# The low parts of projection weights in a split-precision block kernel: an accumulating DMA in place of a VectorE subtraction

## The chip, the cores and the metric

The kernel runs on one core of a Trainium2 chip. The metric is the device time of one execution in microseconds (us); lower is better. The kernel before takes 1429.39 us, the median of 3 runs (1428.5 to 1431.72).

## What is computed

One layer of a diffusion backbone on 1024 latent tokens and 256 context tokens with 1024 channels, all in float32: a modulated norm, one wide input projection `w_in`, a recurrent branch (8 heads) and a Fourier branch, a gated merge, an output projection, and a squared-ReLU MLP. Cut to what matters here:

```python
h_lat = modulate(rms_norm(x, g_mix), sh1, sc1)
ux_l, uy_l, uf_l, ug_l = split_in_cols(h_lat @ w_in)     # 1024 x (1024 | 1024 | 512 | 2048)
xc = depthwise_conv(ux, conv_w, conv_b)                  # per head of 128 channels:
h_l = bidir_rglru(xc_ctx, xc_lat, w_a, b_a, w_x, b_x, lam)   # gates from w_a, w_x, two scans
y_a = (h_l * gelu(uy)) @ w_lru_out
y_b = fourier_mix(uf) @ w_f_out
merged = sigmoid(ug)[:, :1024] * y_a + sigmoid(ug)[:, 1024:] * y_b
x = x + gt1 * (merged @ w_out)
x = x + gt2 * sq_relu_mlp(modulate(rms_norm(x, g_mlp), sh2, sc2), w1, w2)
```

## The kernel before

**Split operands.** The matmuls run on a rounded form of float32 (F32R). To keep the accuracy, each operand is split in two: a high part, which is the operand rounded by a ScalarE copy, and a low part, operand minus high part, by VectorE (`split`, lines 97-98). A product is then three matmul passes into one PSUM bank: weight high by input high, weight high by input low, and, last, weight low by input high (`passes`, line 151). So of each weight, the high part is wanted first and the low part after two passes.

**The stream of weights.** All 60 projection weights up to the merge come through one object, `weights` of class `Stream` (lines 107-137), in the order of the list at lines 139-149:

- four columns `WIN_UF` (the Fourier branch, "the Fourier weights"), seven gates `WIN_GA`, the first convolution weight `win[0]`, and the last `WIN_GA`;
- for each head: `wg` (the head's gate weights, 128 x 512), the convolution weight `win` of the **next** head, `WIN_UY` (the gelu branch), `wf` (Fourier output, 128 x 640), and `WIN_GB`;
- eight columns of `wlo`, the recurrent output projection.

Apart from `wg` and `wf` each is 128 x 1024, 512 KB. `ahead` keeps up to four raw weights loaded (SyncE's DMA queue, line 126, tiles `wr`) and up to three split (tiles `wh` and `wl`, rings of three buffers each); `take` hands out the next and calls `ahead` first. The `wr` ring of four buffers is shared with the gemv of the modulation vectors (`Gemvs.steps`, lines 269-280), which loads rows of `w_mod` there in the heads and multiplies them with VectorE (line 277 the first of a group, line 279 the others). So a weight's load may wait for a gemv step to free its buffer.

**What sets the order.** From line 395 to 443, the start-up, PE, VectorE and ScalarE run in the order in which the code stands (`tc.manual_schedule`): inputs are normalised, transposed and modulated (lines 381-393 hold the helpers), `weights.ahead` at lines 407, 408 and 413 splits the first three Fourier weights, and `uf_mm` (line 420) multiplies each input tile by these three, into the three PSUM buffers named `mm`. Those three buffers are all there are: the fourth Fourier weight is multiplied after it, by `mm_lat` (line 324), once `fourier_in` (line 471, ScalarE) has evacuated the first. Behind the start-up a scheduler sets the order of each engine when the program is built; `take` gives the loads and splits a priority 600 instructions ahead (`PRIO`). Each engine then runs its queue strictly in order, and waits where an operand or buffer is not ready.

**A head.** `gates` (line 613) multiplies the head's convolved input by four gate weights, and ScalarE evacuates each by a tanh (line 626 the latent part, 627 the context part; the context bank `smp` has two buffers, so PE waits at line 622 for 627 two gates before). `conv` of the next head (line 590) runs next on PE, by `lat_mm` (line 321), then `gelu_out` (658), gemv steps, and `fourier_out` (670), whose evacuation by VectorE stands at lines 702 and 703. Scans and gates' products (lines 640-656) are VectorE's.

Of the kernel before, what the change touches and what calls it, by code (L numbers as in the profile page):

```python
# [18 lines left out]
F32R = mybir.dt.float32r  # L19
BF16 = mybir.dt.bfloat16  # L20
I32 = mybir.dt.int32
AF = mybir.ActivationFunctionType
ALU = mybir.AluOpType
# [22 lines left out]
def f32(ap):  # L46
    return ap.bitcast(F32)
# [3 lines left out]
def block_kernel(es: ExitStack, tc: tile.TileContext, a, out):  # L51
    nc = tc.nc
    V, S, PE, G = nc.vector, nc.scalar, nc.tensor, nc.gpsimd
# [21 lines left out]
    def nm(s):  # L75
        uid[0] += 1
        return f"{s}_{uid[0]}"
# [13 lines left out]
    def wr_tile():  # L91
        return wp.tile([P, 1024], F32, tag="wr", name=nm("wr"))
# [4 lines left out]
    def split(src, hi, lo):  # L97
        return S.activation(hi, src, AF.Copy), V.tensor_tensor(lo, src, f32(hi), ALU.subtract)  # L98
# [8 lines left out]
    class Stream:  # L107
# [14 lines left out]
        def ahead(self, split_to=None, load_to=None):  # L122
            while len(self.raw) < min(self.i + 4 if load_to is None else load_to, len(self.items)):
                src, shape = self.items[len(self.raw)]
                r = wr_tile()[:, 0:shape[1] * shape[2]]
                dma(r, src)
                self.raw.append(r)
            while len(self.done) < min(self.i + 3 if split_to is None else split_to, len(self.items)):
                j = len(self.done)
                r, shape = self.raw[j], self.items[j][1]  # L130
                h, l = (wp.tile([P, 1024], F32R, tag=t, name=nm(t), bufs=n)[:, 0:shape[1] * shape[2]]
                        for t, n in (("wh", 3), ("wl", 3)))
                if shape[1] == 5:
                    V.tensor_tensor(r[:, 256:512], r[:, 0:256], r[:, 256:512], ALU.add)
                    V.scalar_tensor_tensor(r[:, 0:256], r[:, 0:256], 2.0, r[:, 256:512], ALU.mult, ALU.subtract)
                split(r, h, l)
                self.done.append([t.rearrange("p (a b) -> p a b", b=shape[2]) for t in (h, l)])

    W8 = (P, KT, P)
# [1251 lines left out]
```

## Time and profile before

| | |
|---|---|
| median of 3 runs | 1429.39 us (1428.5 to 1431.72) |
| profiled execution, its own time | 1429.25 us |
| its span on the core | 1427.4 us |
| mean granted clock of TensorE | 0.993 |
| PE busy (matmul) | 97% |
| VectorE (DVE) busy | 73% |
| ScalarE (ACT) busy | 42% |
| GpSimd (POOL) busy | 1% |
| DMA: by SyncE's queue | 191.53 MB, 38.3% of 16 engines' span |

The profile is of one execution, which took 1429.25 us; the span of its instructions, 1427.4 us, is what timelines and windows cover, counted from the span's start. Busy shares are averages over the whole span, so a place must be read from its own stretch. PEld is the loading of weights into the array beside the matmuls. An idle time is put down to the releaser that came last.

### The profile page before, as it was taken

To read this page: it belongs to the slowest core of one execution; us is meant where nothing else is said; L and a number is where in the kernel's file an instruction comes from. 1 tells how busy PE (TensorE), PEld (TensorE's weight loads), DVE (VectorE), ACT (ScalarE), POOL (GpSimd) and SP (SyncE) were. 2 spreads that over 40 slices of the span, in tenths; PEclk is the share of its full clock that TensorE was granted. 3 is DMA by queue.
4 is the path that set the end of the run, shared out by engine and by line. 5 is a ranking of instruction groups with operands and counts; after the bars stand their busy time and mean duration, and the time that the engine had idled before them with its cause. 6 is when DMAs were issued, how large, how long until landed. Compare 5 with 4: busy or idle time off the path is not lost.

```text
span 1427.4 us, 16255 instructions
## 1 busy us (share of the span) xinstructions
PE 1384.8 (97%) x6352; PEld 1129.5 (79%) x6352; DVE 1046.7 (73%) x1262; ACT 605.3 (42%) x755; POOL 13.8 (1%) x14
## 2 busy tenths in 40 slices
PE   4999999999999999999999899999999999999997
PEld 3888888888888887788877687888887888888885
DVE  7664557898779888854747877666665977969968
ACT  7452337755764666522125612222222544333512
POOL 0000000000000000000000200000000000000000
PEclk9999999999999999999999899999999999999999
DMA  8532711441344135454923233223326561340332
GB/s 336 194 118 67 255 60 60 135 140 66 109 135 134 46 120 171 161 168 164 333 89 133 74 134 132 95 98 118 118 91 238 187 226 63 124 149 1 101 150 104
DMA packets 64556, 192.57 MB, mean 135 GB/s; under 512 B 7203, under 2 KB 7611, under 8 KB 64479
## 3 DMA queue, kind: packets, MB, share of 16 engines
q1 hardware_dynamic: 64479, 191.53, 38.3%
q8 instruction: 50, 0.82, 0.2%
q14 instruction: 27, 0.22, 0.0%
HBM read 154.27 MB, written 37.23 MB: 134 GB/s over the span
## 4 chain that ended last, share of the span: by engine, by line
PE 85%; DVE 7%; ACT 3%; DMA 2%; issue 2%; SPq 0%; DVEq 0%; ACTq 0%
PE mm L321 25%; PE bk L922 19%; PE mm L1141 19%; PE mm L776 6%; PE mm L863 5%; PE mm L1218 3%; PE mm L621 2%; PE smp L596 2%; DVE pg L98 1%; DMA wr<-in_win 1%; ACT jk L217 1%; PE mm L686 1%; PE mm L497 1%; PE smp L622 1%; DVE l L653 1%
## 5 line engine op out<-in xcount | busy, mean ns | idle before, releaser
L321 PE MATMUL mm<-pg,wh 128*128 128x512 f32 x1120 | 309.4, 397 | 0.5 <-DVE pg L98 0.5
L321 PEld LDWEIGHTS mm<-pg,wh 128*128 128x128 f32 x1120 | 205.1, 189 | 43.9 <-DVE pg L98 1.0
L922 PE MATMUL bk<-pg,wh 128*128 128x512 f32 x720 | 228.7, 398 | 4.6 <-DVE pg L98 4.5
L321 PE MATMUL mm<-pg,wl 128*128 128x512 f32 x560 | 175.6, 395 | 0.0
L922 PEld LDWEIGHTS bk<-pg,wh 128*128 128x128 f32 x720 | 136.6, 190 | 38.7 <-DVE pg L98 5.7
L922 PE MATMUL bk<-pg,wl 128*128 128x512 f32 x360 | 143.7, 399 | 0.4 <-DVE wl L98 0.4
L98 DVE TENSOR_TENSOR wl<-wr,wh 128x1024 fp32r<-128x1024 f32 (+2 forms) x73 | 81.6, 1120 | 75.3 <-ACT wh L98 75.1
L98 ACT ACTIVATE wh<-wr 128x1024 fp32r<-128x1024 f32 (+2 forms) x73 | 71.0, 975 | 145.3 <-PE mm L321 67.0
L321 PEld LDWEIGHTS mm<-pg,wl 128*128 128x128 f32 x560 | 105.7, 189 | 24.4
L98 ACT ACTIVATE wh<-pg 128x1024 fp32r<-128x1024 f32 (+1 forms) x52 | 52.7, 1028 | 142.4 <-PE bk L922 52.7
L98 ACT ACTIVATE pg<-pg 128x1024 fp32r<-128x1024 f32 (+4 forms) x93 | 79.4, 884 | 45.8 <-DVE pg L1155 13.2
L98 DVE TENSOR_TENSOR pg<-pg,pg 128x1024 fp32r<-128x1024 f32 (+4 forms) x82 | 77.7, 980 | 24.1 <-ACT pg L98 23.9
L863 PE MATMUL mm<-pg,pg 128*128 128x512 f32 x384 | 92.3, 397 | 0.8 <-DVE g L1016 0.8
L863 PEld LDWEIGHTS mm<-pg,pg 128*128 128x128 f32 x384 | 71.1, 188 | 19.4 <-DVE g L1016 2.8
L922 PEld LDWEIGHTS bk<-pg,wl 128*128 128x128 f32 x360 | 68.5, 190 | 16.9 <-DVE wl L98 0.9
L98 DVE TENSOR_TENSOR wl<-pg,wh 128x1024 fp32r<-128x1024 f32 (+1 forms) x52 | 60.3, 1179 | 21.2 <-ACT wh L98 21.2
L1141 PE MATMUL mm<-pg,pg 128*128 128x512 f32 x240 | 74.1, 390 | 0.0
L776 PE MATMUL mm<-pg,wh 128*128 128x512 f32 x256 | 70.0, 394 | 1.7 <-ACT pg L98 1.7
L1155 DVE TENSOR_TENSOR pg<-pg,mm 128x1024 f32<-128x1024 f32 x34 | 41.0, 1220 | 39.0 <-PE mm L1141 37.8
L922 PE MATMUL bk<-pg,pg 128*128 128x512 f32 x264 | 64.8, 395 | 0.3 <-ACT pg L931 0.3
L1141 PE MATMUL mm<-pg 128*128 128x512 f32 x164 | 64.1, 391 | 0.0
L922 PEld LDWEIGHTS bk<-pg,pg 128*128 128x128 f32 x264 | 49.3, 188 | 12.1 <-ACT pg L931 0.5
(285 smaller groups left out, 2454.7 us busy)
## 6 DMA issues: line engine op xcount, KB each, us to landing
wr<-in_win SPq DMA_DIRECT2D x36, 512.0 KB, 4.5
pg<-act_d SPq DMA_DIRECT2D x70, 256.0 KB, 5.2
pg<-in_wm SPq DMA_DIRECT2D x32, 512.0 KB, 8.2
wr<-in_wm SPq DMA_DIRECT2D x32, 512.0 KB, 3.6
wr<-in_w SPq DMA_DIRECT2D x32, 512.0 KB, 3.5
act_d<-pg SPq DMA_DIRECT2D x32, 512.0 KB, 3.0
pg<-in_w SPq DMA_DIRECT2D x56, 256.0 KB, 5.3
pg<-in_x SPq DMA_DIRECT2D x16, 512.0 KB, 7.9
```

The costliest lines, as they stand in the source:

```text
L98: return S.activation(hi, src, AF.Copy), V.tensor_tensor(lo, src, f32(hi), ALU.subtract)
L217: S.activation(j[:, 0:src.shape[1]], src, AF.Square, accum_out=dst)
L321: PE.matmul(ps[:, h * HB:(h + 1) * HB], l[:, k, :], r[:, h * HB:(h + 1) * HB], start=k == 0 and i == 0, stop=k == KT - 1 and i == 2)
L497: PE.matmul(ps[:, o0:o0 + n1 - n0], l[:, q * P:(q + 1) * P], r[:, n0:n1], start=i == 0, stop=i == 2)
L596: PE.matmul(pc[:, 0:TC], l[:, k, :], r[:, k % 4, :], start=k == 0 and i == 0, stop=k == KT - 1 and i == 2)
L621: PE.matmul(ps[:, h * HB:(h + 1) * HB], l, r[:, h * HB:(h + 1) * HB], start=i == 0, stop=i == 2)
L776: PE.matmul(ps[:, h * HB:(h + 1) * HB], l[:, k, :], r[:, h * HB:(h + 1) * HB], start=k == 0 and i == 0, stop=k == KT - 1 and i == 2)
L863: PE.matmul(ps, l, r, start=k == 0 and j == 0, stop=k == KT - 1 and j == 2)
L922: PE.matmul(ps, l, r, start=first and k == 0 and i == 0, stop=k == 3 and i == 2, skip_group_check=not first)
L1141: PE.matmul(t[j], l, r, start=u not in self.ON and k == 0 and n == 0, stop=k == len(op) - 1 and n == 2, skip_group_check=u in self.ON)
L1155: V.tensor_tensor(t, t, ps, ALU.subtract if u in self.SUB else ALU.add)
L1218: PE.matmul(ps[h], l, r[:, h * HB:(h + 1) * HB], start=f == 0 and j == 0, stop=f == 2 * self.NPL - 1 and j == 2)
```

## The change

For the 52 weights that are not `wf`, the call of `split` is replaced. ScalarE makes the high part as before and then writes the negated weight, rounded the same way, into the low part's tile; a DMA on GpSimd's queue then adds the weight, read from DRAM a second time, onto that tile. The eight `wf`, which are combined by VectorE before they are split, stay as they are. Lines behind the change are five further down.

```diff
@@ Stream.ahead, -133,7 +133,12 @@
                 if shape[1] == 5:
                     V.tensor_tensor(r[:, 256:512], r[:, 0:256], r[:, 256:512], ALU.add)
                     V.scalar_tensor_tensor(r[:, 0:256], r[:, 0:256], 2.0, r[:, 256:512], ALU.mult, ALU.subtract)
-                split(r, h, l)
+                if shape[1] == 5:
+                    split(r, h, l)
+                else:
+                    S.activation(h, r, AF.Copy)
+                    S.activation(l, r, AF.Copy, scale=-1.0)
+                    G.dma_start(out=l, in_=self.items[j][0].rearrange("p a b -> p (a b)").bitcast(F32R), accum_op=ALU.add)
                 self.done.append([t.rearrange("p (a b) -> p a b", b=shape[2]) for t in (h, l)])
```

In the whole program VectorE loses 52 instructions (`TENSOR_TENSOR wl<-wr,wh`, 44 of 128x1024 and 8 of 128x512), ScalarE gains 52 of the same sizes, and POOL's queue gains 52 transfers of 512 KB (8 of them 256 KB).

ScalarE in the start-up, where the first three Fourier weights are split (`wr` raw weight, `wh` and `wl` its high and low part; `pg<-smp,mod` is the modulation of an input tile). Before:

```order
L98 ACTIVATE wh_292<-wr_171 128x1024
L98 ACTIVATE wh_296<-wr_173 128x1024
L388 ACTIVATE pg_310<-smp_282,mod 128x512
L98 ACTIVATE pg_95<-pg_310 128x512
L388 ACTIVATE pg_310<-smp_283,mod 128x512
L98 ACTIVATE pg_95<-pg_310 128x512
L98 ACTIVATE wh_328<-wr_175 128x1024
L388 ACTIVATE pg_335<-smp_318,mod 128x512
```

With the change, the same stretch:

```order
L139 ACTIVATE wh_292<-wr_171 128x1024
L140 ACTIVATE wl_293<-wr_171 128x1024
L139 ACTIVATE wh_297<-wr_173 128x1024
L140 ACTIVATE wl_298<-wr_173 128x1024
L393 ACTIVATE pg_312<-smp_282,mod 128x512
L98 ACTIVATE pg_95<-pg_312 128x512
L393 ACTIVATE pg_312<-smp_283,mod 128x512
L98 ACTIVATE pg_95<-pg_312 128x512
L139 ACTIVATE wh_330<-wr_175 128x1024
L140 ACTIVATE wl_331<-wr_175 128x1024
L393 ACTIVATE pg_338<-smp_320,mod 128x512
```

Each high part has its negation right behind it; two operations stand ahead of the first modulation, and three ahead of that of the second input tile.

ScalarE at the end of the start-up, where the fourth Fourier weight (`wr_599` before, `wr_602` now) is split and the three PSUM buffers `mm` are evacuated by `fourier_in` (line 471, now 476). Before:

```order
L98 ACTIVATE wh_603<-wr_599 128x1024
L471 ACTIVATE pg_662<-mm_342 128x1024
L98 ACTIVATE wh_609<-wr_601 128x1024
L98 ACTIVATE wh_670<-wr_607 128x1024
L471 ACTIVATE pg_664<-mm_343 128x1024
L471 ACTIVATE pg_666<-mm_344 128x1024
```

With the change:

```order
L139 ACTIVATE wh_606<-wr_602 128x1024
L140 ACTIVATE wl_607<-wr_602 128x1024
L139 ACTIVATE wh_613<-wr_604 128x1024
L139 ACTIVATE wh_675<-wr_611 128x1024
L140 ACTIVATE wl_614<-wr_604 128x1024
L140 ACTIVATE wl_676<-wr_611 128x1024
L476 ACTIVATE pg_667<-mm_345 128x1024
L476 ACTIVATE pg_669<-mm_346 128x1024
L476 ACTIVATE pg_671<-mm_347 128x1024
```

The first evacuation stood behind one split; it now stands behind the splits and negations of three weights.

VectorE in head 1, around the first gemv step of the head (`gacc<-wr,silu`, line 277, now 282), which frees a `wr` buffer (`l<-l,mm` at 128x255 to 257 is the evacuation of `fourier_out`, lines 702 and 703, now 707 and 708). Before:

```order
L662 SCALAR_TENSOR_TENSOR l_2022<-l_2022,mm_1973 128x1024
L656 TENSOR_TENSOR l_1849<-l_1849,l_1856 128x1024
L702 TENSOR_TENSOR l_2079<-l_2079,mm_2066 128x257
L703 TENSOR_TENSOR l_2079<-l_2079,mm_2066 128x255
L702 TENSOR_TENSOR l_2079<-l_2079,mm_2066 128x256
L703 TENSOR_TENSOR l_2079<-l_2079,mm_2066 128x256
L664 SCALAR_TENSOR_TENSOR l_2022<-l_2022,mm_1973 128x1024
L277 TENSOR_SCALAR gacc<-wr_2029,silu 128x1024
```

With the change:

```order
L661 TENSOR_TENSOR l_1865<-l_1865,l_1872 128x1024
L98 TENSOR_TENSOR l_1980<-l_1970,l_1979 128x1280
L667 SCALAR_TENSOR_TENSOR l_2039<-l_2039,mm_1990 128x1024
L282 TENSOR_SCALAR gacc<-wr_2046,silu 128x1024
L707 TENSOR_TENSOR l_2097<-l_2097,mm_2084 128x257
L708 TENSOR_TENSOR l_2097<-l_2097,mm_2084 128x255
L707 TENSOR_TENSOR l_2097<-l_2097,mm_2084 128x256
L708 TENSOR_TENSOR l_2097<-l_2097,mm_2084 128x256
L284 SCALAR_TENSOR_TENSOR gacc<-wr_2049,silu,gacc 128x1024
```

The first gemv step stood behind the four rows of the Fourier evacuation, and now stands ahead of them; the same in the other heads that have gemv steps.

## Rows read from the trace of the kernel before

**Rows 1.** Page, part 1: busy time, share of the span, instructions of each engine.

```profile
PE 1384.8 (97%) x6352; PEld 1129.5 (79%) x6352; DVE 1046.7 (73%) x1262; ACT 605.3 (42%) x755; POOL 13.8 (1%) x14
```

**Rows 2.** Windows: length, busy PE, PEld, DVE, ACT, POOL, then PEclk, DMA share, GB/s.

```profile
35.00:75.00 40.00, 39.48 (x206) 32.64 (x205) 25.86 (x42) 17.82 (x23) 0.00 (x0) 1.00 0.45 173
...
215.00:580.00 365.00, 361.11 (x1808) 301.61 (x1808) 305.33 (x294) 234.99 (x260) 0.00 (x0) 1.00 0.34 113
580.00:700.00 120.00, 118.29 (x510) 95.28 (x509) 71.55 (x78) 31.46 (x44) 0.00 (x0) 1.00 0.59 203
```

**Rows 3.** Waits of PE from 35 to 700 us: total, times, longest.

```profile
PE smp L622 <- ACT l L627: 2.6, 3, 1.5
PE mm L776 <- ACT pg L98: 1.7, 1, 1.7
PE smp L622 <- DVE wr L297: 1.3, 1, 1.3
```

**Rows 4.** Costs by line and form: count | busy, mean ns | idle before, releaser.

```profile
L98 DVE TENSOR_TENSOR wl<-wr,wh 128x1024 fp32r<-128x1024 f32 x57 | 69.5, 1222 | 67.2 <-ACT wh L98 67.0 <-DMA pg<-in_wm 0.2
L98 ACT ACTIVATE wh<-wr 128x1024 fp32r<-128x1024 f32 x57 | 60.1, 1057 | 120.1 <-DMA wr<-in_win 52.4 <-PE mm L321 41.8 <-issue 12.1
```

**Rows 5.** Page, part 6: DMA issues, KB each, median us to landing.

```profile
wr<-in_win SPq DMA_DIRECT2D x36, 512.0 KB, 4.5
...
pg<-in_wm SPq DMA_DIRECT2D x32, 512.0 KB, 8.2
wr<-in_wm SPq DMA_DIRECT2D x32, 512.0 KB, 3.6
```

**Rows 6.** Timeline of ACT, 24 to 50: start, us, instruction, [idle before].

```profile
26.35 1.99 ACT L98 ACTIVATE wh<-wr 128x1024 fp32r<-128x1024 f32 x2
30.22 0.78 ACT L388 ACTIVATE pg<-smp,mod 128x512 f32<-128x512 f32 x1 [1.87 <-DVE mod L261]
...
32.89 1.04 ACT L98 ACTIVATE wh<-wr 128x1024 fp32r<-128x1024 f32 x1
```

**Rows 7.** Timeline of PE, 24 to 50.

```profile
33.14 2.06 PE L321 MATMUL mm<-pg,wh 128*128 128x512 f32 x4
...
35.67 1.09 PE L321 MATMUL mm<-pg,wh 128*128 128x512 f32 x4
...
38.01 0.63 PE L321 MATMUL mm<-pg,wl 128*128 128x512 f32 x2
```

**Rows 8.** Timeline of ACT, 72 to 80.

```profile
73.67 1.06 ACT L98 ACTIVATE wh<-wr 128x1024 fp32r<-128x1024 f32 x1 [3.00 <-PE mm L321]
74.63 1.01 ACT L471 ACTIVATE pg<-mm 128x1024 f32<-128x1024 f32 x1
```

**Rows 9.** Timeline of PE, 73 to 79.

```profile
76.67 1.10 PE L321 MATMUL mm<-pg,wh 128*128 128x512 f32 x4
77.61 0.63 PE L321 MATMUL mm<-pg,wl 128*128 128x512 f32 x2
```

**Rows 10.** Timeline of ACT in head 1.

```profile
261.76 1.06 ACT L98 ACTIVATE wh<-wr 128x1024 fp32r<-128x1024 f32 x1 [6.95 <-DMA wr<-in_win]
```

**Rows 11.** Timeline of PE in head 1, the convolution's first low pass.

```profile
271.30 0.63 PE L321 MATMUL mm<-pg,wl 128*128 128x512 f32 x2
```

**Rows 12.** Timeline of DVE in head 1.

```profile
254.76 0.42 DVE L702 TENSOR_TENSOR l<-l,mm 128x257 f32<-128x257 f32 x1
...
257.21 0.75 DVE L277 TENSOR_SCALAR gacc<-wr,silu 128x1024 f32<-128x1024 f32 x1
```

**Rows 13.** Windows around a stop of PE behind the stretches above; columns of rows 2.

```profile
804.90:808.20 3.30, 0.00 (x0) 0.00 (x0) 3.30 (x4) 2.16 (x3) 1.65 (x1) 0.80 0.00 0
808.20:817.10 8.90, 7.66 (x17) 5.59 (x18) 7.23 (x10) 1.12 (x2) 0.00 (x0) 0.50 0.70 236
```

**Rows 14.** Timeline of PE, 591 to 598.

```profile
594.68 1.19 PE L776 MATMUL mm<-pg,wh 128*128 128x512 f32 x4 [1.71 <-ACT pg L98]
```

**Rows 15.** Timeline of DVE, 24 to 46.

```profile
38.48 1.53 DVE L249 SCALAR_TENSOR_TENSOR gacc<-pg,silu,gacc 128x512 f32<-128x512 f32 x2
```

## The prediction, made before the changed kernel had run

> **What bounds the kernel now.** I read the busy shares first, then the stretches in which the changed weights are used, then the costs of the operation removed, then the waits and timelines at the places where a low part is needed soonest. TensorE is busy for 97% of the span, VectorE for 73% and ScalarE for 42% [rows 1]. The stretches that use the 52 changed weights are fuller still: PE is busy for 39.48 of 40 us in the start-up, 361.11 of 365 in heads 1 to 6 and 118.29 of 120 with the last eight weights, while VectorE has 305 of 365 at most [rows 2]. So PE sets the time there, and VectorE is a helper with room. All the idle time of PE that a lighter VectorE could give back in these stretches is 0.5 + 3.9 + 1.7 = 6 us, and most of it waits for ScalarE: 2.6 us for the gate evacuation and 1.7 for a split, against 1.3 in the largest row for VectorE [rows 3].
>
> **What the change removes and adds.** One VectorE subtraction of a full weight takes 1.22 us [rows 4]; 44 such and 8 of half the size make about 59 us less work for VectorE. Since PE waits so little for VectorE in these stretches, I cost this gain at nothing: it is hidden under PE, which remains full. ScalarE gets one more operation per weight, 1.06 us each by the row of the first [rows 4], about 51 us in all; it has 130 of 365 us free in the heads [rows 2], so in bulk that is hidden too, and it costs only where a released buffer or a PSUM bank stands behind it. The third part is new: 52 transfers on POOL's queue, 24 MB read a second time. In the heads that is four weights a head, 1.8 MB in some 60 us or 30 GB/s, beside the 113 GB/s there at a DMA share of 0.34 [rows 2], so bandwidth in bulk is hidden as well. What remains is latency: a low part is ready when the negation has ended **and** the accumulating transfer has landed, instead of 1.22 us after the high part.
>
> **The unknown, X**: from the end of the negation to the landing. No row of before shows a transfer issued by POOL, or one that adds. The nearest rows are plain loads of the same 512 KB from SyncE: median 3.6 us where little else runs, 4.5 for the weights themselves, 8.2 in the crowded start-up [rows 5]. The lower bound is 3.6, since it must move the same bytes. As upper bound I take 12: one read of the source and one of the destination before the write, so more than twice 4.5, with some issue time on POOL. I take 7, half as much again as the weight load, because it is nearest to that row; in the start-up burst 8.2.
>
> By the Trainium skill, "Collectives: The Full Stack", section "The bandwidth ceiling", an adding transfer is slower than a copy because it needs two source reads, not because of the sum. If that doubled the whole 4.5 us, X would be 9, and the sum below would be 19 instead of 16.3; no run here shows it yet.
>
> **(a) Start-up, third weight.** Here PE begins the projections as soon as inputs exist, and all three Fourier weights are split moments before. ScalarE's third split starts at 32.89 [rows 6]; the two extra negations ahead of it go almost wholly into the 1.87 us idle there (first order excerpt), so the high part is ready at 33.9 and the negation at about 35.0. Landing at 35.0 + 8.2 = 43.2. PE wants that low part at 38.01 [rows 7]: 5.2 us late; 1.5 at X = 4.5, 9.0 at 12. The first two weights (negations end near 28.4 and 30.4 by the pace of the two splits from 26.35 [rows 6]; wanted near 35.2 and 36.7, when the matmuls ahead of them end [rows 7]) are less late than that at each X, and since PE takes the three in order the delays do not add: the largest counts.
>
> **(b) The fourth weight**, the last Fourier one. Its buffers come free only as PE finishes the first weight, so the split starts at 73.67 and the low part is wanted at 77.61, 3.9 us later [rows 8, 9]. With the change: high part 74.7, negation 75.7, landing 82.7 at X = 7: 5.1 us late. There is a floor that does not hang on X. PE's first matmul of this weight needs a PSUM bank that the first evacuation (line 471) frees, at 74.63 now [rows 8]. In the new order that evacuation stands behind six ScalarE operations instead of one (second excerpt): 73.67 plus six of about 1.0 and its own 1.0 is about 80.7, against PE's start at 76.67 [rows 9]. That is 4.0 us late even for a free transfer, and 10.1 at X = 12, where the landing at 87.7 decides. At X = 7 the two overlap: the larger counts, 5.1.
>
> **(c) The convolution weights of the heads**, in heads 1 to 6, are the only ones split late: in head 1 the split starts at 261.76, when its load has landed after 6.95 us of waiting [rows 10], and the low part is wanted at 271.30 [rows 11]. Two ScalarE operations leave 7.4 us. But the gemv step whose end frees that load's buffer now stands ahead of four other VectorE operations (third excerpt), so it can start near 254.76 rather than 257.21 [rows 12], and the load comes about 2.4 us sooner: a budget near 9.9 us. At X = 7 it costs nothing, covered by the gates' matmuls; at 12 it is 2.1 x 6 = 12.6 us. The other 40-odd weights are split 14 us or more ahead of their first low pass, by my count over the trace of their splits and matmuls, and cost nothing.
>
> **(d) ScalarE's queue in the heads.** The negations stand ahead of the gate evacuations, for which PE waits 2.6 us already in three places [rows 3]. I estimate half a microsecond in seven heads, 3.5 us, less the 2.6 if the removed VectorE work lets the gates start in better step: +1, with bounds -2.6 and +5.
>
> **(e) The clock.** After PE stood still for 3.3 us at 804.9 the granted clock was 0.50 (1.2 GHz) for the next 8.9 us, 7.66 of them busy, about 3.8 us lost [rows 13]. At 33.14 a restart after small work took 2.06 us for four matmuls that need 1.09 later, about 1 us lost [rows 7]. After an idle of 1.71 us at 594.68 four took 1.19: hardly anything lost [rows 14]. Two stalls of 4 us or more lie above; between the rows at 1 and at 3.8 I take 2.5 us each, 5 in all, with bounds 0 and 8.
>
> **Sum:** 5.2 + 5.1 + 0 + 1 + 5 = 16.3 us slower. The profiled execution itself took 1429.25 us, 1.85 over its span and level with the median of 1429.39, so the forecast is **1446 us**.
>
> **Rivals.**
> *The transfer is as quick as a plain load*, X = 4.5. Then (a) is 1.5, (b) its floor 4.0, (c) 0, (d) 1, and the clock loses 2.5 in one stall: +9, **1438 us**. For it: the queue has little else, and POOL is idle (1% busy). Against: it reads twice and its issue is not free. The Trainium skill, "DMA: Bandwidth & Descriptors", section "Anatomy of one DMA — SWDGE (gpsimd) path", gives 2.0 us plus the bytes over 436 GB/s, an estimate of 3.2 us for 512 KB, by which the time would lie here; no row of before can bear it out.
>
> *The transfer is slow*, X = 12: 9.0 + 10.1 + 12.6 + 1 + 6 = +39, **1468 us**. From about 10 on, the heads decide. Against: plain loads stay under 8.2 even when crowded [rows 5].
>
> *The issue on POOL waits for VectorE.* If the descriptors could be written only while VectorE is idle, the third weight would start at 40.0, the end of VectorE's row of work there [rows 15], and land at 47: (a) is 9, (b) 5, and with the rest about **1455 us**. No row of before speaks for it or against it, since no transfer there is issued by POOL. The Trainium skill, "SBUF — State Buffer", section "SBUF: two separate sides", tells of such a block by VectorE operations in a two-port mode; the subtractions and gemv steps here have two inputs and are not of that kind.
>
> *Not slower.* VectorE's removed 59 us gives back PE's 6 us of idle time, X stays below 3, so that (a) vanishes, and ScalarE is early enough at 73.67 for the floor of (b) to shrink below what is regained: about **1427 us**, deciding from X = 3 and a split at 70. Against: the idle time is not VectorE's [rows 3], ScalarE there waits for PE itself [rows 8], and an X under 3 is shorter than any of the plain loads [rows 5].
>
> **How the numbers follow.** The forecast has a chance of 0.47, the quick transfer 0.25, the slow one 0.15, the waiting issue 0.06, no loss 0.07. The range reaches from 1433 (the quick transfer with no clock loss and the 2.6 us of gate waits regained: 1.5 + 4.0 + 1 - 2.6 = 4) to 1470, just past the slow case at X = 12; above lies an X of 13 and more. A difference of 0.2%, 2.9 us, is about what a measurement of this kernel can tell from none. Faster by more than that: 0.03. Within it: 0.07, the rest of the no-loss case and the lowest edge of the quick one. Slower: 0.90.
>
> **What would show it right or wrong.** VectorE should lose 52 operations and about 59 us, ScalarE gain 52 and 51 us, with PE's span no shorter for it. PE should stand idle before the low pass of the third weight near 38, for X - 3, and from about 77, first for the evacuation, then for the low part; the heads from 215 to 580 should keep their length. The transfers' time from issue to landing is X itself: over 10 us, and PE would wait for a transfer ahead of every convolution. If PE showed no wait at 38 and 77, or the span were shorter, the reasoning would be wrong at its root; if a wait for VectorE appeared in the heads, I would have missed a reordering.

## The result and the profile after

The changed kernel takes 1479.16 us, the median of 3 runs (1478.17 to 1484.47), against 1429.39 before: a ratio of 1.0359, 95% interval [1.0345, 1.0373], so 50 us slower. The profiled execution is the slowest of the three, 1484.47 us; its times run some 5 us past the median by the end, so its stretches add up to 55 us and not to 50.

Page of the changed kernel, part 1, to compare with [rows 1]:

```profile
PE 1406.4 (95%) x6352; PEld 1142.1 (77%) x6352; DVE 992.6 (67%) x1210; ACT 650.8 (44%) x807; POOL 59.0 (4%) x66
```

VectorE has lost 52 instructions and 54 us (59 was worked out), ScalarE has gained 52 and 45.5 us (51), and the whole span grew. Windows of the same stretches, which lie some 22 us later at the first head and 55 at the last, to compare with [rows 2]:

```profile
35.00:87.00 52.00, 45.00 (x220) 36.11 (x220) 28.75 (x45) 22.64 (x28) 1.82 (x3) 0.93 0.52 171
...
237.00:635.00 398.00, 373.73 (x1808) 309.30 (x1807) 272.47 (x261) 257.79 (x284) 25.18 (x29) 0.96 0.53 136
635.00:757.00 122.00, 119.67 (x515) 96.24 (x514) 66.33 (x74) 40.80 (x56) 6.94 (x8) 1.00 0.78 238
```

The start-up takes 52 us instead of 40. Between it and the heads 10 us more are lost (150 us instead of 140), by the rest of the fourth weight and by the context's vectors, which are made there. The heads take **398 us instead of 365**: 33 of the 55 us of this execution, where the forecast had one. PE stands idle there for 24 us instead of 4, and is busy 12.6 us longer for the same work at a granted clock of 0.96 instead of 1.00. The last eight weights take 2 us more; the rest of the kernel is 2 us shorter. PE's longest waits from 35 to 757, as in [rows 3]:

```profile
PE smp L627 <- ACT l L632: 14.5, 5, 5.9
PE mm L626 <- ACT l L722: 8.6, 3, 3.7
PE mm L326 <- DMA wl<-in_win: 6.2, 4, 2.2
PE smp L261 <- DVE gacc L254: 5.0, 3, 2.3
PE mm L781 <- DMA wl<-in_wlo: 2.3, 1, 2.3
PE mm L326 <- ACT pg L476: 1.4, 1, 1.4
```

**The start-up** went as worked out. PE's rows before the low parts of the first three weights, then the fourth weight (to compare with [rows 7, 9]):

```profile
36.59 0.73 PE L326 MATMUL mm<-pg,wl 128*128 128x512 f32 x2 [1.68 <-DMA wl<-in_win]
...
40.42 0.73 PE L326 MATMUL mm<-pg,wl 128*128 128x512 f32 x2 [2.16 <-DMA wl<-in_win]
...
44.22 1.22 PE L326 MATMUL mm<-pg,wl 128*128 128x512 f32 x2 [1.58 <-DMA wl<-in_win]
...
49.35 0.95 PE L261 MATMUL smp<-ones,gacc 128*128 128x1 f32 x8
...
88.52 1.64 PE L326 MATMUL mm<-pg,wh 128*128 128x512 f32 x4 [1.42 <-ACT pg L476]
90.92 1.22 PE L326 MATMUL mm<-pg,wl 128*128 128x512 f32 x2 [0.77 <-DMA wl<-in_win]
```

The small matmuls of L261 stand behind the slow ones; in the kernel before they started here:

```profile
41.27 0.95 PE L256 MATMUL smp<-ones,gacc 128*128 128x1 f32 x8
```

The third low part's first pass starts at 44.22 instead of 38.01, 6.2 us late, and 8.1 us have been lost once the slow matmuls behind it are done (49.35 against 41.27). The fourth weight starts at 88.52 instead of 76.67, 3.8 us more, and its low pass at 90.92 instead of 77.61, another 1.5. Behind each stall four matmuls take 1.6 to 1.9 us instead of 1.1; when they are done, at 96.07 instead of 80.38, 15.7 us have been lost. ScalarE and POOL tell the fourth weight's story (to compare with [rows 6, 8]); first ScalarE:

```profile
83.68 1.99 ACT L139 ACTIVATE wh<-wr 128x1024 fp32r<-128x1024 f32 x2
85.57 1.99 ACT L140 ACTIVATE wl<-wr 128x1024 fp32r<-128x1024 f32 x2
87.47 2.83 ACT L476 ACTIVATE pg<-mm 128x1024 f32<-128x1024 f32 x3
```

then POOL, whose row is the issue of the adding transfer:

```profile
35.16 0.86 POOL L141 DMA_DIRECT2D wl<-in_win  x1 [3.67 <-ACT wl L140]
84.07 0.86 POOL L141 DMA_DIRECT2D wl<-in_win  x1 [48.05 <-ACT wl L140]
```

and VectorE at the first of them:

```profile
33.62 2.32 DVE L254 SCALAR_TENSOR_TENSOR gacc<-pg,silu,gacc 128x512 f32<-128x512 f32 x3
```

The evacuations (L476) begin at 87.47, behind the six operations, and PE at once behind the first. Transfers of the changed kernel: the share of the DMA engines' time that POOL's queue took, then count, size and median us from issue to landing (to compare with [rows 5]):

```profile
q0 software_dynamic: 7488, 25.17, 9.4%
...
wl<-in_win POOLq DMA_DIRECT2D x36, 512.0 KB, 7.8
...
pg<-in_wm SPq DMA_DIRECT2D x32, 512.0 KB, 10.0
...
z_d<-l SPq DMA_DIRECT2D x7, 512.0 KB, 8.1
```

X is 7.8. The row that the prediction never looked at is the last: `z_d<-l`, the **store** of a head's gelu product (`gelu_out`, line 667 before, 672 now). It takes 8.1 us to land; before, the same view says:

```profile
z_d<-l SPq DMA_DIRECT2D x7, 512.0 KB, 3.9
```

**A head.** SyncE's queue in head 2 of the kernel before:

```profile
305.45 0.33 SPq L126 DMA_DIRECT2D wr<-in_win  x1
306.59 0.33 SPq L667 DMA_DIRECT2D z_d<-l  x1
307.79 0.33 SPq L126 DMA_DIRECT2D wr<-in_win  x1
```

and of the changed kernel:

```profile
329.62 3.98 SPq L126 DMA_DIRECT2D wr<-in_win  x2
335.28 0.33 SPq L126 DMA_DIRECT2D wr<-in_wf  x1
335.70 0.38 SPq L126 DMA_DIRECT2D wr<-in_win  x1
336.92 0.33 SPq L126 DMA_DIRECT2D wr<-in_wg  x1
337.30 0.87 SPq L672 DMA_DIRECT2D z_d<-l  x1
```

The store stood behind one load of the group; it now stands behind all five, and these wait for `wr` buffers. The operation of VectorE that makes the product ended at 306.56 before, 0.03 us ahead of the store; now it ends at 334.37, and the store is issued 2.9 us later (1.6 or 2.9 in heads 1 to 6):

```profile
333.15 1.22 DVE L670 SCALAR_TENSOR_TENSOR l<-l,l 128x1024 f32<-128x1024 f32 x1
```

The chain of what ended last, from there to PE (start, us, what):

```profile
336.92 0.33 SPq L126
337.24 0.05 issue
337.30 8.07 DMA z_d<-l
...
345.45 1.02 ACT l L722
346.47 0.37 ACT l L632
346.85 0.04 issue
346.89 0.58 PE smp L627
```

The tanh at line 722 (717 before; the gate of `fourier_out`) writes a tile that has two buffers, and its buffer is the one that the store reads. So the tanh waits for the landing, and gate evacuations (lines 631 and 632) stand behind it on ScalarE. ScalarE waits six times for this store in the heads, 24.8 us:

```profile
ACT l L722 <- DMA z_d<-l: 24.8, 6, 5.8
```

Before, 1.9 us in three times:

```profile
ACT l L717 <- DMA z_d<-l: 1.9, 3, 0.9
```

### The profile page after: what moved, and what is told of

Read it like the earlier page. It is cut to its first block, busy times and chain, and to the rows that moved or that the text cites. A ratio compares the mean times of both kernels' runs of the same rounds, so it can differ in the third digit from the quotient of the medians.

```text
span 1482.7 us, 16425 instructions
## 1 busy us (share of the span) xinstructions
PE 1406.4 (95%) x6352; PEld 1142.1 (77%) x6352; DVE 992.6 (67%) x1210; ACT 650.8 (44%) x807; POOL 59.0 (4%) x66
## 4 chain that ended last, share of the span: by engine, by line
PE 75%; DMA 8%; DVE 8%; issue 6%; ACT 3%; SPq 0%; DVEq 0%; ACTq 0%; POOLq 0%
PE bk L927 19%; PE mm L1146 18%; PE mm L326 17%; PE mm L781 6%; PE mm L868 5%; DMA z_d<-l 3%; PE mm L1223 3%; PE mm L626 2%; PE smp L601 2%; DVE gacc L284 1%; DVE pg L98 1%; DMA pg<-in_wm 1%; DMA wl<-in_win 1%; PE mm L691 1%; PE smp L627 1%
## 5 line engine op out<-in xcount | busy, mean ns | idle before, releaser
L326 PEld LDWEIGHTS mm<-pg,wh 128*128 128x128 f32 x1120 | 207.2, 191 | 46.2 <-ACT pg L476 1.5
L139 ACT ACTIVATE wh<-wr 128x1024 fp32r<-128x1024 f32 (+1 forms) x52 | 51.4, 991 | 119.2 <-PE mm L326 58.9
L781 PEld LDWEIGHTS mm<-pg,wh 128*128 128x128 f32 x256 | 48.1, 188 | 11.7
```

The costliest lines, as they stand in the source:

```text
L139: S.activation(h, r, AF.Copy)
L326: PE.matmul(ps[:, h * HB:(h + 1) * HB], l[:, k, :], r[:, h * HB:(h + 1) * HB], start=k == 0 and i == 0, stop=k == KT - 1 and i == 2)
L781: PE.matmul(ps[:, h * HB:(h + 1) * HB], l[:, k, :], r[:, h * HB:(h + 1) * HB], start=k == 0 and i == 0, stop=k == KT - 1 and i == 2)
```

## The experiments

Three theories of the heads went into the first runs, and with them the start-up terms of the prediction. **S**: the store's place on SyncE's queue. **A**: the extra ScalarE operations. **C**: contention with the second reading of the weights. Times stand against the kernel before on the same chip, 1429.1 to 1430.3 us.

**e1, the store first.** `after(op)` makes what is inside issue behind op.

```diff
-                dma(r, src)
+                with after(*self.behind):
+                    dma(r, src)
...
-                dma(z_d[hd], t)
+                weights.behind = [dma(z_d[hd], t)]
```

> The changed kernel, with the store of the gelu product (z_d) put ahead of the following weight loads on SyncE's queue, as it stands ahead of all but one of them before the change. Theory S (in the heads the store is issued behind five loads instead of one, lands late, and the tanh that needs its buffer holds up the gate evacuations and so PE): the 33 us that the heads grew by go away, 1450 us, between 1443 and 1456. Theory A (the 52 extra ScalarE operations delay the evacuations): 1474 or more. Theory C (the second reading of the weights slows all other transfers, the store from 4 to 8 us): about half, 1460 to 1468.

1472.84 us, ratio 1.0302 [1.0286, 1.0317]: only 6 us back, which none of the theories had said. The store now lands in 3.0 us, but the loads stand behind it, and the convolution's low parts come late in its place. PE's waits (3.3 us of the first row in the start-up, where the expectation of e8 puts 5.4; L724 is the tanh, two lines further down here):

```profile
PE mm L328 <- DMA wl<-in_win: 15.4, 7, 3.5
...
PE mm L628 <- ACT l L724: 3.3, 3, 1.2
```

Moving the store ahead is thus no clean undoing of its lateness; that took e13, e15 and e16.

**e2, the four Fourier weights alone.**

```diff
-                if shape[1] == 5:
+                if shape[1] == 5 or j >= 4:
```

> The change for the four Fourier weights of the start-up alone; the other 48 low parts by VectorE, so the order of the heads is that of before. The start-up terms, as the profile after shows them (7.4 us at the first three weights, 8.3 at the fourth, clock included), come to 15.7: all three theories expect 1445, between 1441 and 1448. If later stages took some of it back: 1432 to 1440.

1444.02 us, ratio 1.0103 [1.0088, 1.0118]: +14.8. The start-up terms stand, and none of it is taken back later. (Their split into 7.4 and 8.3 is wrong: by the rows above it is 8.1 and 7.6; the sum is the same.)

**e3, the negation without the transfer.** ScalarE still writes the negation, then VectorE the low part over it.

```diff
-                    G.dma_start(out=l, in_=..., accum_op=ALU.add)
+                    V.tensor_tensor(l, r, f32(h), ALU.subtract)
```

> The changed kernel without the transfer: ScalarE makes the high part and the negation, and VectorE then writes the low part over the negation, so ScalarE has its 52 extra operations, no byte is read twice and VectorE has its old work. The store stands behind two to four loads on SyncE's queue here. Theory A: 33 us in the heads and the 4 us floor of the fourth weight, 1466. Theory C: 1430 to 1435. Theory S: between, 1435 to 1455, by where the store stands, and PE's waits lie behind the tanh that waits for the store.

1439.17 us, ratio 1.0067 [1.005, 1.0084]. The 52 operations of ScalarE cost 10 us and not 37, and in the trace some 9 of them are lost ahead of the first head, so theory A by itself falls for the heads. The largest of PE's waits in it is the floor of the fourth weight, where the evacuation stands behind six operations although nothing is transferred:

```profile
PE mm L326 <- ACT pg L476: 3.6, 1, 3.6
```

**e4, the negation by VectorE,** the transfer kept.

```diff
-                    S.activation(l, r, AF.Copy, scale=-1.0)
+                    V.tensor_scalar(l, r, -1.0, None, ALU.mult)
```

> The changed kernel with the negation made by VectorE instead of ScalarE, the transfers unchanged. ScalarE has its old 730 instructions; the store stands behind three or four loads instead of five. Theory A: the heads are as before, about 1446. Theory S: the most of the loss stays, 1455 to 1472. Theory C: 1475 to 1482.

1474.6 us, ratio 1.0313 [1.0297, 1.0328]: 45 us over before with ScalarE unburdened (755 instructions, as before), just above the range of S and just under that of C. Most of the loss doesn't need A; as the order is another one here too (the store behind two to four loads), this run doesn't say more.

**e5 and e6, transfers for which nobody waits,** in the kernel before, whose other engines keep their order.

```diff
                 split(r, h, l)
+                if shape[1] != 5:
+                    G.dma_start(out=shadow[j % 8][:, 0:shape[1] * shape[2]], in_=l)
```

e6 has `accum_op=ALU.add` besides.

> The kernel before, each engine in its order of before; on POOL's queue each of the 52 low parts, once made by VectorE, is also copied to a DRAM scratch that nobody reads, 512 KB each as in the change, plain. Nothing waits for these transfers. Theory C-any (a further 512 KB in flight, whatever its kind, slows the stores and loads beside it): 1440 or more. Theory C-add (only an adding transfer does): 1428 to 1433. Theory L (the loss is the low parts' own lateness and the new order): 1428 to 1433 too.

> The same, but the 52 transfers add onto the DRAM scratch instead of overwriting it. Nothing waits for them. Theories C-add and C-any: the store of the gelu product lands some 4 us later in each of seven heads where an adding transfer flies beside it, 1440 to 1460. Theory L: 1428 to 1433.

1435.78 us, ratio 1.0038 [1.0025, 1.0051], and 1446.47, ratio 1.0121 [1.0104, 1.0138]: 6 and 17 us. The first lies under the range of "any transfer" and above that of "adding only"; both were too simple: plain stores cost a little, adding ones nearly three times as much. Yet the heads grew by 1 to 2 us in e6; most of it lies where the context's vectors are made: between the two timelines the same matmuls are shifted by 1.9 us at 148 and by 12.6 at 189. The first of PE's waits in e6 belongs there (L259 is line 256 of the kernel before):

```profile
PE smp L259 <- DVE gacc L252: 4.6, 2, 2.4
```

The store is still behind one load there. So contention is a cost of its own, but not what the heads lost.

**e7, a plain copy in the changed kernel** (`accum_op` left out, so the low part is the whole weight and the subtraction is missing), and **e10**, the same with the store first.

> The changed kernel with a plain copy where the adding transfer was, same queue, tile, source and order of every engine (the low part is then the whole weight, so the output is not the reference's: the subtraction is left out). Theory C-add: the copy lands in 4 to 5 us instead of 7.8, the store beside it in about 4 instead of 8; start-up loses about 8 instead of 15.7 and the heads at most half of 33: 1440 to 1455. Theory C-any: 1470 to 1480, with the copy as slow as the addition. Theory L with the order alone (store behind five loads): 1455 to 1470.

> Run e1 (store first) with a plain copy where the adding transfer was (the subtraction is left out, so the low part is the whole weight). Start-up 10 and the context's vectors 5, as in run e7; if the heads lose by the store's place on the queue and by the adding transfer's length, and by nothing else, they lose 4 to 8 here: 1447 to 1454. If the store's place costs nothing with a plain copy: as e7, 1457 to 1462. If e1's late low parts stay: 1460 to 1468.

1459.99 us, ratio 1.0211 [1.0194, 1.0228], and 1453.1, ratio 1.0155 [1.0131, 1.0179]. The copy lands in 5.8 us and takes 5.3% of the engines' span where the addition takes 7.8 us and 9.4%:

```profile
q0 software_dynamic: 7488, 25.17, 5.3%
...
wl<-in_win POOLq DMA_DIRECT2D x36, 512.0 KB, 5.8
```

The adding is worth 19 of the 50 us. e7 loses 7 us more than e10, but in the two traces 4 of these are there at the first head already (16 us behind the kernel before against 12), ahead of the first of these stores: in the heads themselves e7 loses 20 us and e10 18. So with plain copies, too, moving the store ahead gives little back there.

**e8, e12 and e9, which weights.** e12 keeps the four Fourier and eight convolution weights on VectorE, e8 is e12 with the store first, e9 has the change for the eight convolution weights alone.

```diff
+    conv_w = [11] + [14 + 5 * h for h in range(KT - 1)]
...
-                if shape[1] == 5:
+                if shape[1] == 5 or j < 4 or j in conv_w:
```

(e9: `shape[1] == 5 or j not in conv_w`.)

> The changed kernel with the store ahead of the loads, and the low parts of the four Fourier and the eight convolution weights made by VectorE as before; 40 adding transfers are left, on weights that are split far ahead. Run e1 with those waits taken out: there PE waited 15.4 us for low parts of w_in weights, 5.4 of it in the start-up. If the late low parts and the late store are the whole loss: 1430 to 1436. If the adding transfers slow the loads of the convolution weights and of the context's vectors beside them: 1440 to 1455.

> Run e8 without the forced order: the low parts of the four Fourier and eight convolution weights by VectorE, 40 adding transfers, and the store behind two to four loads, where the queue's order puts it. Against e8 at 1437.5: if the store's place costs 2 to 4 us a head when adding transfers fly, 1448 to 1462; if the convolution's low parts are what decides, 1435 to 1441.

> The change for the eight convolution weights alone (52 less 44); the store stands on SyncE's queue as in the kernel before. If a low part that comes late by its own chain (load, two ScalarE operations, 8 to 9 us of adding transfer) is a cost of the heads by itself: 1.5 to 3 us in each of six or seven heads, 1439 to 1450. If it was late in run e1 only because other adding transfers flew beside it: 1429 to 1434.

e8 1437.48 us, ratio 1.0063 [1.0048, 1.0078]; e12 1433.28, ratio 1.0027 [1.0018, 1.0037]; e9 1433.88, ratio 1.003 [1.0021, 1.0039]. e8 lies between its two cases, e12 just under both of its own, and e9 in its second: without other adding transfers these low parts are hardly late. Added up, 4 weights alone cost 14.8 us (e2), 8 alone 4.5, the 40 others alone 3.9, together 23; all 52 at once cost 50. The other 27 come from something that needs the convolution weights' transfers and others together.

**e13 and e14, what meets what.** In a burst of a head two adding transfers fly, of the convolution and of the gelu weight. e13 takes the gelu weights (and the four Fourier ones) out, and keeps the store behind five loads; e14 has the change for convolution and gelu weights alone, with the store behind one load or none.

```diff
+    uy_w = [15 + 5 * h for h in range(KT - 1)] + [49]
...
-                if shape[1] == 5:
+                if shape[1] == 5 or j < 4 or j in uy_w:
```

(e14: `shape[1] == 5 or j not in conv_w + uy_w`.)

> The change without the four Fourier and the eight gelu weights (their low parts by VectorE): 40 adding transfers, among them those of the convolution weights, and the store behind five loads as in the changed kernel, but only one adding transfer in the burst of a head. Theory S (the store behind five loads beside the convolution weight's adding transfer): the heads lose 25 or more, 1456 to 1470. Theory P (two adding transfers in the burst): 1433 to 1441.

> The change for the eight convolution and the eight gelu weights alone, so both adding transfers are in a head's burst, while the store stands on SyncE's queue behind no or one load, as in the kernel before. Theory P: 1452 to 1465. Theory S: 1431 to 1441.

e13 1468.46 us, ratio 1.026 [1.0243, 1.0277]; e14 1444.77, ratio 1.0096 [1.0078, 1.0114]. e13 loses 38 us with one adding transfer in the burst, so theory S stands. e14's 14.5 is more than S alone gave and less than P, so two adding transfers in a burst cost as well, by low parts that come late (PE waits 8.9 us for them). In e13 the wait is where S has it; PE's longest:

```profile
PE mm L628 <- ACT l L724: 20.5, 6, 4.3
```

**e15 and e16, the store's place alone.** e15 is e13 with the edit of e1. e16 is the whole changed kernel with the store on another queue:

```diff
-                dma(z_d[hd], t)
+                S.dma_start(z_d[hd], t)
```

> Run e13 (1468.5) with the store put ahead of the loads. If the store's place on SyncE's queue is the cause of the loss in its heads: 1434 to 1443. If the adding transfer alone makes the store or another wait late: 1455 to 1468.

> The whole changed kernel, with the store issued from ScalarE's queue instead of SyncE's. If the store's lateness is the most of the heads' loss and the loads keep their times of the changed kernel: 1446 to 1458. If the two adding transfers make the convolution's low part late whenever the store isn't (as in e1): 1462 to 1474.

e15 1449.37 us, ratio 1.014 [1.0123, 1.0157]; e16 1456.63, ratio 1.019 [1.0175, 1.0206]. e15 lies between its two cases: it gives back half of e13's 38 us. The store lands in 3.0 us instead of 8.1, and of the other half 11 us are lost in the heads, where PE now waits 6.7 us for low parts whose loads stand behind the store. e16 neither delays the loads nor waits for them: on SyncE's queue they keep the order of the changed kernel, without the store. Its windows of the heads and of the last eight weights:

```profile
238.00:604.00 366.00, 361.85 (x1802) 300.85 (x1802) 272.53 (x261) 255.41 (x286) 25.19 (x29) 1.00 0.57 148
604.00:730.00 126.00, 122.20 (x521) 98.27 (x520) 65.66 (x73) 41.30 (x55) 6.95 (x8) 0.99 0.73 230
```

The heads take 366 us again, with all 52 transfers in flight, the negations on ScalarE, and PE busy for 361.85. ScalarE's wait for the store there:

```profile
ACT l L722 <- DMA z_d<-l: 1.5, 1, 1.5
```

So **the store's turn on SyncE's queue made nearly the whole loss of the heads**, in this order and with these transfers in flight. It is not the flight alone: in e16 the store is issued 0.03 us behind its product in head 2, and still takes a median of 6.7 us to land:

```profile
z_d<-l ACTq DMA_DIRECT2D x7, 512.0 KB, 6.7
```

Nor is it the place alone: in e7, with the order of the changed kernel on every engine and plain copies, the heads lose 20 us. Read from the first gate matmul of the first head to the first matmul of the last eight weights, the profiles say what the heads lose against the kernel before: the changed kernel 33 us, e13 32, e1 26, e7 20, e4 and e10 18, e15 11, e16 2.5, e3 and e12 less than 1. (The profiled executions of the changed kernel, e7 and e10 are 4 to 5 us slower than their medians. By medians e16 gives back 22.5 of the 50 us.)

What e16 still loses, 27.5 us, lies outside the heads for the most part: the start-up with 14.8 (e2), and 13 mostly at the context's vectors and the last eight weights, where PE waits for a gemv step and for a low part:

```profile
PE smp L261 <- DVE gacc L254: 6.3, 3, 2.8
...
PE mm L781 <- DMA wl<-in_wlo: 3.8, 1, 3.8
```

**e11, the kernel before with its store first** (the edit of e1).

> The kernel before with its store ahead of the loads, no other change. If the store is what PE's waits for the gate evacuations (2.6 us) come from there too: 1425 to 1428. If those waits are ScalarE's own: within 2 us of 1429.5.

1428.67 us, ratio 0.9992 [0.9983, 1.0002]: no difference that can be told. In the kernel before the store was nearly on time, and no version beat it.

## Why the prediction was wrong

The direction was right and the range missed by 9 us: 1479 against 1433 to 1470.

- **X** was taken as 7 and 8.2 in the start-up; from issue to landing it is 7.8, and 9.1 for the third weight (35.16 to a first pass at 44.22). The rival of the quick transfer falls, and so does the slow one at 12, whose total is near the measured one for another reason. By the Trainium skill, "Collectives: The Full Stack", section "The bandwidth ceiling", an adding transfer needs two source reads; the runs agree as to the engines' time (9.4% against 5.3% for the same bytes), while the time to landing grew by a third only. The estimate of 3.2 us from the Trainium skill, "DMA: Bandwidth & Descriptors", section "Anatomy of one DMA — SWDGE (gpsimd) path", is too short here: the plain copy took 5.8 among the kernel's other traffic.
- **The issue that waits for VectorE** did not happen: POOL issued the third transfer at 35.16, in the middle of VectorE's work from 33.62 to 35.94, and PE's pass behind it started 9.1 us later, where the second, issued at 30.62, took 9.8. These operations of VectorE have two inputs; the first of each gemv group has one, and no row here tells of that. By its own terms (9 + 5 + 1 + 5) this rival would have come to 1449, not 1455.
- **(a)** 5.2 was worked out, 6.2 measured. **(b)** 5.1 was worked out; PE's start slipped by 3.8 and its low pass by 1.5 more, 5.2. The floor of 4.0 is shown by e3, where PE waits 3.6 us for the evacuation with no transfer at all. **(e)** 5 was taken; the slow matmuls behind the two stalls added 1.9 and 2.4, 4.3. Together 15.3 worked out, 15.7 in the profile, 14.8 in e2.
- **(c)** "At X = 7 it costs nothing" was near: the eight convolution weights alone cost 4.5 (e9), and in e16 all of the 6.1 us that PE waits for low parts of `w_in` lie in the start-up.
- **VectorE's gain at nothing** was right: with 54 us less work of VectorE, no stretch of [rows 2] became shorter.
- **(d) is the step that failed**: "+1, with bounds -2.6 and +5". It costed what stands on ScalarE's own queue, and e3, whose heads lose less than 1 us, shows that this was a fair price for it. It did not ask what else the evacuations wait for. The tanh ahead of them waits for a store, that store for its turn on SyncE's queue, and the new order put four more loads ahead of it. The third excerpt showed half of this: the gemv step that moved ahead frees the loads' buffers sooner. I booked it as a gain of 2.4 us for the convolution's load under (c), and never read on that queue what stood behind the loads. That this gemv step is what moved the store back on the queue is argued from the orders and was not tested. With the store late, the term is 33 us in the profile and not 1. The prediction's sign of a missed reordering was a wait for VectorE in the heads; this one showed as waits for ScalarE, 14.5 and 8.6 us.
- **"Bandwidth in bulk is hidden"** was wrong too: adding transfers for which nobody waits cost 17 us (e6), 11 of them where the context's vectors are made. Their loads, `pg<-in_wm`, rose from a median of 8.2 to 10.0 us [rows 5]; but in e2 they took 9.8 and nothing was lost there, so the median alone doesn't tell why. The 27.5 us that e16 loses are 12 more than (a), (b) and (e), some 8 of them at the context's vectors.
- **The other 40-odd weights**, taken at nothing, do cost at the first of the last eight: PE waits 2.3 us for its low part, and 3.8 in e16. The loads of these eight took a median of 8.1 us (7.4 in e16) where it had been 3.5.

## What to carry to other kernels

When a change alters a scheduled order, read **every** queue near each wait, the queue of the loads and stores above all, and ask for each tile with few buffers which transfer frees it. A chain with hardly any slack (1.9 us of waiting in seven heads before) turns the delay of one store into the delay of every engine behind it. Effects of parts can be far from additive (23 against 50 here), so take out a part in several ways before naming a cause. To test a queue's order, move the transfer to another queue; moving it ahead can shift the lateness to what it passes (e1).

## What was not expected of the hardware

- An adding transfer takes 1.8 times the DMA engines' time of a plain one of the same size (9.4% against 5.3%), and idle ones cost 17 us where idle plain stores cost 6.
- A 512 KB store took 3.0 us when it was issued ahead of the loads (e1), and 8.1 when three loads were issued within 2.0 us before it and an adding transfer flew beside it. In head 2 its flight was some 4 us longer than the median before (8.1 against 3.9), and its wait on the queue was 2.9; yet issued in time (e16), with 6.7 us of flight, it held up the heads hardly at all.
